# Two layers of a diffusion backbone: the transposes of the attention weights wait for the last head of their block

## The chip, the cores and the metric

The kernel runs on one core of one Trainium2 chip. Its engines are TensorE (PE, with a queue of its own for loading the stationary operand, PEld), VectorE (DVE), ScalarE (ACT), GpSimd (POOL) and SyncE (SP), each of which works through its own list of instructions; DMA queues move the data. The metric is the device time of one execution in microseconds (us), the median of several runs.

## The reference

The program computes two layers over 512 latent tokens and 256 context tokens of width 1024, in single precision. Layer 0 mixes tokens by attention, layer 1 by a bidirectional retention; each is followed by a SwiGLU feed-forward part, and all parts are modulated by a condition vector. The change lies in the attention of layer 0. Sixteen query heads share four key heads. Latent tokens are taken in blocks of 128 queries; a block attends in one softmax to its window of up to 384 latent keys, to all 256 context keys, and to one learned sink value per head:

```python
s_ctx = jnp.einsum('bqkgd,bnkd->bkgqn', qb, k_c, preferred_element_type=jnp.float32) * scale
s_loc = jnp.einsum('bqkgd,bnkd->bkgqn', qb, kb, preferred_element_type=jnp.float32) * scale
s_loc = jnp.where(valid, s_loc, NEG_INF)
sink_col = jnp.broadcast_to(sink_g, s_ctx.shape[:-1] + (1,))
p = jax.nn.softmax(jnp.concatenate([s_ctx, s_loc, sink_col], axis=-1), axis=-1).astype(vb.dtype)
return (jnp.einsum('bkgqn,bnkd->bqkgd', p[..., :L], v_c)
        + jnp.einsum('bkgqn,bnkd->bqkgd', p[..., L:L + band], vb))
```

Context tokens attend to the 256 context keys and the sink alone.

## The kernel before

The attention stage runs over four groups g of four query heads that share a key head, and in each group over six blocks: four of latent queries and two of context queries, 24 blocks in all. `attend(g, s, b)` (line 757) issues one block: `score(i)` for its four heads, `turn(ki)` for each of its two to five key tiles of 128 keys, then `output()`.

- `score(i)`. POOL copies the head's sink value into the last column of a row buffer `pr` (line 687). PE multiplies queries and keys into a PSUM bank (line 703; every product takes two matmuls). DVE adds the mask, stores the row and keeps its extreme (line 704). After each second head DVE scales the extremes of the pair (line 710), ACT takes the exponentials of both rows and sums them (line 101), DVE inverts the sums (line 714), and POOL multiplies each row by its inverse (line 717): this is the normalisation. A block so has two pairs of heads and four normalisations.
- `turn(ki)`. PE transposes the 128 columns of key tile ki of the four rows into one PSUM bank `pT`, of which there are two (line 726). The first of the four transposes takes head 0, then follow heads 2, 1 and 3. ACT or DVE, in turn, copies the bank to SBUF as `tt` (line 728).
- `output()`. PE multiplies the values by `tt`, two products a key tile (line 740). The first ones wait for the last copy of the block, by a dependency that the program states itself (line 742). DVE copies the result out (line 755), or in the last group ACT and DVE split it in two parts at once (lines 164 and 165).

Row buffers: nine of `pr`, so two blocks and one head are in flight; a buffer is free for line 687 of a later block when the last transpose of its row is done.

Between the blocks of a group stand the pieces of `make_q` (lines 559 to 632), which project the queries of the next group: 48 matmuls per pair of heads over the latent and the context tokens (lines 147 to 149). In the last group the output projection of the context tokens stands there instead. They have nothing to do with the block beside them and can fill PE while it waits for a softmax.

The order of each engine's list in this stage is not written out by hand. A planner takes the instructions in the program's order as their rank, follows the dependencies, and puts on each engine what it takes to be ready at that time. An instruction that is ready early by its account, such as the transpose of head 0, is placed early, and on the chip the engine then waits at it for whatever is late. The stages before and after have the same order in both programs.

Of the kernel before, what the change touches and what calls it, by code (L numbers as in the profile page):

```python
# [14 lines left out]
P = 128  # L15
# [34 lines left out]
def dit_kernel(ctx, tc, xT, cT, crow, small, consts, masks, tabs0, tabs1, jtab, adaQ, adaN, adaT, wst, out):  # L50
    nc = tc.nc
    mult, add, sub = ALU.mult, ALU.add, ALU.subtract
# [9 lines left out]
    def T(pool, cols, tag, bufs, dt=F32):  # L62
        return pool.tile([P, cols], dt, tag=tag, bufs=bufs, name=tag)
# [8 lines left out]
    ident, bd = cst[:, 0:128], cst[:, 128:256]  # L72
# [27 lines left out]
    def lnexp(*args, **kw):  # L100
        ins = nc.scalar.activation(*args, **kw)  # L101
        after(ins, [turn["pre"]])
        turn["lnexp"].append(ins)
        return ins
# [150 lines left out]
    def gated_add(s, l, part, d, o, res):  # L255
        return nc.vector.scalar_tensor_tensor(res[d], o, mods[l, s][:, part, d:d + 1], res[d], mult, add)  # L256
# [407 lines left out]
    run_dep = mybir.DependencyInfo(mybir.DependencyClass.Sync, mybir.DependencyReason.DATA)  # L664
# [3 lines left out]
    class Block:  # L668
# [9 lines left out]
        def score(self, i):  # L678
            g, s, b, n = self.g, self.s, self.b, len(self.keys) * P
            hd, nl = 4 * g + i, len(self.lk) * P  # L680
            if i % 2 == 0:
                self.st = T(ap, 16, "stat", 4)
            st, c = self.st, 2 * (b + 4 * s)
            qt = q[hd, s][:, b * P:(b + 1) * P]
            pt = T(ap, 656, "pr", PRB)[:, :n + 1]
            top = stats[hd][:, 1, c + hd % 2:c + hd % 2 + 1]
            nc.gpsimd.tensor_copy(pt[:, n:n + 1], top)
            lo, x0 = st[:, i % 2:i % 2 + 1], self.lk[0] * P if nl else 0

            if nl == 384:  # L690
                runs = [(nl, SC, 5 * P, [(0, SC, kc)]), (0, nl, 2 * P, [(0, nl, kx)])]
            elif nl == 0:
                runs = [(0, SC, 5 * P, [(0, SC, kc)])]
            elif b == 0:
                runs = [(0, n, 3 * P, [(0, nl, kx), (nl, SC, kc)])]
            else:
                runs = [(0, n, 0, [(0, SC, kc), (SC, nl, kx)])]
            for c0, w, m0, parts in runs:
                bank = pS()[:, :w]
                for p0, pw, kk in parts:  # L700
                    for r in range(2):
                        keys = kk[g][r] if kk is kc else kk[g][r][:, x0:x0 + pw]
                        nc.tensor.matmul(bank[:, p0:p0 + pw], qt, keys, start=r == 0, stop=r == 1)  # L703
                nc.vector.tensor_tensor_reduce(pt[:, c0:c0 + w], bank, mask[:, m0:m0 + w], 1.0, top, add, ALU.min, lo)
                top = lo
            self.pr.append(pt)
            if i % 2 == 0:
                return
            y = stats[hd][:, 0, c:c + 2]
            nc.vector.scalar_tensor_tensor(st[:, 2:4], st[:, 0:2], -1.0, y, mult, mult)  # L710
            for e in range(2):
                pt = self.pr[i - 1 + e]
                lnexp(pt, pt, AF.Exp, scale=y[:, e:e + 1], bias=st[:, 2 + e:3 + e], accum_out=st[:, 4 + e:5 + e])
            nc.vector.reciprocal(st[:, 6:8], st[:, 4:6])  # L714
            for e in range(2):
                pt = self.pr[i - 1 + e]
                nc.gpsimd.tensor_scalar(pt[:, :n], pt[:, :n], st[:, 6 + e:7 + e], 1.0, op0=mult, op1=mult)  # L717
            if i == 3:
                self.tt = []

        def turn(self, ki):
            if ki >= len(self.keys):
                return
            tp = pT()
            for a in range(4):
                nc.tensor.transpose(tp[:, a * P:(a + 1) * P], self.pr[(0, 2, 1, 3)[a]][:, ki * P:(ki + 1) * P], ident)  # L726
            tt = T(ap, 512, "tt", TTB)
            self.last = nc.scalar.copy(tt, tp) if ki % 2 == 0 else nc.vector.tensor_copy(tt, tp)
            if ki % 2 == 0:
                self.copy = self.last  # L730
            self.tt.append(tt)
# [83 lines left out]
    def context_out(d, w):  # L815
        o = pj(SC)
        project(w, o_t[1], o)
        ins = gated_add(1, 0, 2, d, o, cres)
        add_square(1, int(d != early[0]), cres[d])
        return ins  # L820
# [37 lines left out]
    for d4 in range(0, KT, 4):  # L858
# [4 lines left out]
        for d in range(d4, d4 + 4):  # L863
            o = pj(SX)
            project(w[d - d4], o_t[0], o)
            ins = gated_add(0, 0, 2, d, o, xr)
# [3 lines left out]
        for d in range(d4, d4 + 4) if d4 else ():  # L870
            ins = context_out(d, w[d - d4])
# [142 lines left out]
    def seven():  # L1014
        g, u = raw_turn(), raw_turn()
        l_, r_ = slice(0, 512), slice(512, 1024)
        b11 = w_parts(fp, 1)
        split(g, *b11)
        t1 = T(fp, 512, "bhi", 1, F32R), T(fp, 512, "blo", 1, F32R)
        nc.vector.tensor_tensor(g[:, l_], u[:, l_], g[:, l_], op=sub)  # L1020
        split(g[:, l_], *t1)
        nc.vector.tensor_tensor(g[:, l_], u[:, r_], g[:, l_], op=sub)
        nc.vector.tensor_tensor(g[:, r_], g[:, r_], g[:, l_], op=sub)
        b24 = w_parts(fp, 1)
        half = split(g, *b24)
        nc.vector.tensor_tensor(u[:, l_], u[:, r_], u[:, l_], op=sub)
        b3 = w_parts(fp, 1)
        split(u, *b3)
        if cr:
            ada_next(half)  # L1030
        X, Y, Z = bank("X"), bank("Y"), bank("Z")
        c11, c12, c22, c21 = t_hn(384), t_hn(384), t_sq(384), t_sq(384)
        a = new_act()
        product(Y, operand["11"], b11, 0, True)
        nc.scalar.copy(c11, Y)
        product(X, operand["12"], b11, 512, True)
        nc.vector.tensor_tensor(c11, c11, X, op=add)
        silu(c11, c11)
        product(Y, operand[2], b24, 0, False)
        nc.scalar.copy(c12, Y)  # L1040
        product(Z, operand[1], t1, 0, True)
        nc.scalar.copy(c21, Z)
        product(Y, operand[3], b3, 0, False)
        nc.scalar.copy(c22, Y)  # L1044
        nc.vector.tensor_tensor(c22, c22, c21, op=add)
        product(Z, operand[4], b3, 512, False)
        nc.vector.tensor_tensor(c12, c12, Z, op=add)
        finish_half(a, 0, c11, c12)
        product(Y, operand["22"], b24, 512, False)
        silu(c21, Y)  # L1050
        return a, finish_half(a, 1, c21, c22)
# [74 lines left out]
    for gsz in FFN_GROUPS:  # L1126
        acts = []
        for i in range(gsz):
# [4 lines left out]
            else:  # L1133
                if f == PLAIN:
                    last_sum()
                a, end = seven()
# [178 lines left out]
    def first_weights_v(hd):  # L1315
        return [split_chunk(chunk(chunk_base + 16 * hd + 4 + i)) for i in range(2)]

    def values_first(w, by_k=False):

        Y = [W4("Z"), W4("Z")]  # L1320
        ins = product_v(Y, quarter_of("11"), w, True, by_k=by_k)
        vt = [T(rp, 512, "res", 12) for _ in range(4)]
        for t in range(2):
            nc.scalar.copy(vt[t], Y[t])
        return w, Y, vt, ins
# [10 lines left out]
    b11, Yv, vt, ins = values_first(b11, True)  # L1336
    normed = context_norm([ins])
    for hd in range(RH):
# [236 lines left out]
        if not last:  # L1575

            b11, Yv, vt, ins = values_first(first_weights_v(hd + 1))
# [7 lines left out]
        def out_tile(d, c, tags="XY"):  # L1585
            while len(w) * 2 <= d:
                w.append(next_w(hpool[0]))
            oo = (W4(tags[d % 2]) if tags[d % 2] != "j" else pj())[:, c]
            for k in range(4):
                c0 = k * 256 + (d % 2) * P  # L1590
                mm3(oo, [p[c0 // 512][:, c0 % 512:c0 % 512 + P] if type(p) is list else p[:, c0:c0 + P]
                         for p in w[d // 2]],
                    (yt[k][0][:, c], yt[k][1][:, c]), k == 0, k == 3)
            return nc.vector.scalar_tensor_tensor(xr[d][:, c], oo, mods[1, 0][:, 2, d:d + 1], xr[d][:, c], mult, add)
# [38 lines left out]
        for i, c in ((0, HALVES[1]), (1, HALVES[0])):  # L1633
            for d in range(KT):
                ins = out_tile(d, c, "XY" if i else "jZ")
# [283 lines left out]
```

## Time and profile before

| what | value |
|---|---|
| median of 3 runs | 1748.62 us (1747.97 to 1750.29) |
| span of the profiled execution, first to last instruction | 1744.4 us |
| instructions in it | 27605 |
| first and last transpose (line 726) | 108.1 us, 315.4 us |
| DMA, mean | 117 GB/s |

The profiled execution is one run, and the page gives its span; the times of runs are taken from outside of it and are 4.2 us longer in the median. In the rows that follow, times are in us unless marked ns; a row of a timeline gives the start, the length, engine, line, operation, what it writes and reads, and in brackets how long the engine stood idle before it and for whom it waited. The ends of matmuls are modelled and overlap the next one, so how fast PE really goes is read from start to start. A row of waits gives the sum, the count and the longest. A row of windows gives, for a stretch, its length and each engine's busy time with its count of instructions, then the granted clock of PE as a share, the share of DMA and its GB/s.

### The profile page before, as it was taken

Reading aid. Unit: us, or ns where it says so; the run is one execution under the profiler, and the core shown is the slowest. Engines: PE = TensorE matmul, PEld = TensorE weight load, DVE = VectorE, ACT = ScalarE, POOL = GpSimd, SP = SyncE. Lnnn points to the kernel's source line nnn. Section 1 sums busy time; section 2 is a strip of 40 time slices with the busy share of each in tenths; the row PEclk is TensorE's granted clock in tenths of the full one; section 3 lists DMA queues with packets and bytes.
Section 4 is the critical chain, followed back from the end, with each engine's and each line's share of the span. In section 5 each row is a group of like instructions: output and inputs, shape, how many; then the busy total and the mean of one; then the engine's idle time right before and its main releaser. Section 6 shows DMA issues by size and latency. Waiting matters only on the chain.

```text
span 1744.4 us, 27605 instructions
## 1 busy us (share of the span) xinstructions
PE 1712.7 (98%) x10876; PEld 1527.8 (88%) x10876; DVE 1350.5 (77%) x2368; ACT 846.3 (49%) x1492; POOL 131.0 (8%) x270
## 2 busy tenths in 40 slices
PE   7999999999999999999999999999999999999999
PEld 5777777899999999999988888898898899999997
DVE  6697778788778788787889858758768798777774
ACT  5576667465433334342456534525525565445442
POOL 0035435000000000000000000000000000000000
PEclk9999999999999999999999999999999999999999
DMA  9501012533243534343423524423423224233322
GB/s 353 230 13 38 13 43 68 204 122 135 71 147 121 158 109 145 123 153 101 156 99 86 182 84 130 162 86 121 157 85 118 76 84 132 77 117 101 104 79 85
DMA packets 59602, 203.54 MB, mean 117 GB/s; under 512 B 6608, under 2 KB 6992, under 8 KB 59216
## 3 DMA queue, kind: packets, MB, share of 16 engines
q1 hardware_dynamic: 51984, 175.03, 30.9%
q0 software_dynamic: 7200, 26.22, 5.2%
q8 instruction: 85, 1.39, 0.3%
q10 hardware_dynamic: 288, 0.52, 0.1%
q14 instruction: 45, 0.37, 0.1%
HBM read 199.65 MB, written 2.10 MB: 116 GB/s over the span
## 4 chain that ended last, share of the span: by engine, by line
PE 80%; DVE 8%; DMA 5%; ACT 3%; issue 2%; POOL 1%; SPq 0%; ACTq 0%; POOLq 0%; DVEq 0%
PE Y L886 15%; PE Z L886 7%; PE pj L147 6%; PE pj L148 6%; PE pj L149 6%; PE Z L1268 6%; PE X L886 4%; PE Y L1257 3%; PE pj L1268 2%; PE pT L726 2%; PE X L1257 2%; DMA wraw<-in_wst_dram 2%; PE pO L740 2%; PE S L703 2%; DMA adan<-in_adaQ_dram 1%
## 5 line engine op out<-in xcount | busy, mean ns | idle before, releaser
L164 ACT CAST whi<-wraw 128x1024 fp32r<-128x1024 f32 x258 | 270.2, 1051 | 370.7 <-PE Z L149 88.5
L165 DVE TENSOR_TENSOR wlo<-wraw,whi 128x1024 fp32r<-128x1024 f32 x258 | 315.0, 1223 | 60.9 <-ACT whi L164 59.7
L886 PE MATMUL Y<-aq,whi 128*128 128x384 f32 x640 | 173.7, 335 | 0.5 <-ACT sq L1044 0.5
L256 DVE SCALAR_TENSOR_TENSOR res<-pj,mod,res 128x512 f32<-128x512 f32 (+1 forms) x112 | 81.5, 729 | 65.6 <-PE pj L149 65.0
L886 PEld LDWEIGHTS Y<-aq,whi 128*128 128x128 f32 x640 | 116.6, 188 | 1.7 <-ACT sq L1044 0.9
L273 DVE CUSTOM_DVE_ANT_0 y<-adaw,crow,small_sb 128x1024 bf16<-128x1024 f32 x64 | 81.9, 1280 | 36.0 <-DMA adaw<-in_adaT_dram 35.7
L886 PE MATMUL Y<-aq,wlo 128*128 128x384 f32 x320 | 107.0, 334 | 0.0
L101 ACT ACTIVATE pr<-pr,stat,qs 128x513 f32<-128x513 f32 (+2 forms) x96 | 74.4, 777 | 23.5 <-DVE stat L710 22.9
L1268 PE MATMUL Z<-whi,sA 128*128 128x512 f32 x256 | 81.0, 391 | 1.2 <-ACT gate L1454 1.2
L717 POOL TENSOR_SCALAR pr<-pr,stat 128x512 f32<-128x512 f32 (+2 forms) x96 | 70.2, 744 | 79.5 <-DVE stat L714 54.8
L147 PE MATMUL pj<-ax,whi 128*128 128x512 f32 x176 | 68.8, 391 | 0.1
L149 PE MATMUL pj<-ax,whi 128*128 128x512 f32 x176 | 68.7, 390 | 0.0
L148 PE MATMUL pj<-ax,wlo 128*128 128x512 f32 x176 | 68.5, 389 | 0.0
L147 PE MATMUL pj<-act,whi 128*128 128x512 f32 x168 | 66.0, 393 | 0.0
L148 PE MATMUL pj<-act,wlo 128*128 128x512 f32 x168 | 65.9, 392 | 0.0
L149 PE MATMUL pj<-act,whi 128*128 128x512 f32 x168 | 65.5, 390 | 0.0
L270 POOL DMA_DIRECT2D adaw<-in_adaT_dram x48 | 25.6, 533 | 514.9 <-DVE mod L273 413.6
L726 PE MATMUL pT<-const_sb,pr 128*128 128x128 f32 x352 | 57.4, 285 | 6.1 <-POOL pr L717 3.6
L886 PE MATMUL Y<-sA,whi 128*128 128x256 f32 x304 | 60.6, 282 | 0.2 <-ACT res L1721 0.2
L886 PEld LDWEIGHTS Y<-aq,wlo 128*128 128x128 f32 x320 | 60.1, 188 | 0.0
L726 PEld LDWEIGHTS pT<-const_sb,pr 128*128 128x128 f32 x352 | 39.1, 142 | 23.0 <-POOL pr L717 12.4
L1268 PEld LDWEIGHTS Z<-whi,sA 128*128 128x128 f32 x256 | 48.0, 188 | 11.7 <-ACT gate L1454 1.9
(576 smaller groups left out, 5150.3 us busy)
## 6 DMA issues: line engine op xcount, KB each, us to landing
wraw<-in_wst_dram SPq DMA_DIRECT2D x224, 512.0 KB, 3.7
adaw<-in_adaT_dram POOLq DMA_DIRECT2D x48, 512.0 KB, 3.9
wx<-in_wst_dram SPq DMA_DIRECT2D x30, 512.0 KB, 4.3
adan<-in_adaQ_dram SPq DMA_DIRECT2D x16, 512.0 KB, 8.5
adan<-in_adaN_dram SPq DMA_DIRECT2D x12, 512.0 KB, 7.8
adaw<-in_adaT_dram SPq DMA_DIRECT2D x8, 512.0 KB, 3.9
res<-in_xT_dram SPq DMA_DIRECT2D x14, 256.0 KB, 3.8
aq<-in_adaN_dram SPq DMA_DIRECT2D x12, 256.0 KB, 5.8
```

What stands on the lines that cost most here:

```text
L101: ins = nc.scalar.activation(*args, **kw)
L147: nc.tensor.matmul(o, whi, xhi, start=first, stop=False)
L148: nc.tensor.matmul(o, wlo, xhi, start=False, stop=False)
L149: return nc.tensor.matmul(o, whi, xlo, start=False, stop=last)
L164: after(nc.scalar.copy(hi, t), behind)
L165: return nc.vector.tensor_tensor(lo, t, hi, op=sub)
L256: return nc.vector.scalar_tensor_tensor(res[d], o, mods[l, s][:, part, d:d + 1], res[d], mult, add)
L273: res.append(nc.vector.tensor_tensor_reduce(junk, w, cr[:, s * 1024:(s + 1) * 1024], 1.0, sm_t[:, C_ADAB + l * 48 + j:C_ADAB + l * 48 + j ...
L726: nc.tensor.transpose(tp[:, a * P:(a + 1) * P], self.pr[(0, 2, 1, 3)[a]][:, ki * P:(ki + 1) * P], ident)
L886: nc.tensor.matmul(o, p, r, start=first and k + i == 0, stop=k == 3 and i == 2, skip_group_check=not first)
L1257: ins = nc.tensor.matmul(o[:, e * SC:(e + 1) * SC], p[:, ws], r, start=first and k + e + i == 0, stop=k == 3 and i == 2, skip_group_check= ...
L1268: ins = nc.tensor.matmul(os[t], p, r, start=first and k + i == 0, stop=k == 3 and i == 2, skip_group_check=by_k or not first)
```

## The change

The last normalisation of a pair is remembered, and each transpose gets a dependency on the one remembered when `turn` is issued, which is that of the block's fourth head. Arithmetic, buffers and the order in which the program issues its instructions stay as they are; the planner makes a new order from them.

```diff
@@ -714,7 +714,7 @@
             nc.vector.reciprocal(st[:, 6:8], st[:, 4:6])
             for e in range(2):
                 pt = self.pr[i - 1 + e]
-                nc.gpsimd.tensor_scalar(pt[:, :n], pt[:, :n], st[:, 6 + e:7 + e], 1.0, op0=mult, op1=mult)
+                self.normed = nc.gpsimd.tensor_scalar(pt[:, :n], pt[:, :n], st[:, 6 + e:7 + e], 1.0, op0=mult, op1=mult)
             if i == 3:
                 self.tt = []
 
@@ -723,7 +723,8 @@
                 return
             tp = pT()
             for a in range(4):
-                nc.tensor.transpose(tp[:, a * P:(a + 1) * P], self.pr[(0, 2, 1, 3)[a]][:, ki * P:(ki + 1) * P], ident)
+                ins = nc.tensor.transpose(tp[:, a * P:(a + 1) * P], self.pr[(0, 2, 1, 3)[a]][:, ki * P:(ki + 1) * P], ident)
+                tc.add_manual_dep(ins.ins, self.normed.ins.name, run_dep, reason="transposes of a tile in one run")
             tt = T(ap, 512, "tt", TTB)
```

`run_dep` (line 664) is the kind of dependency that `output()` uses already: it orders two instructions on different engines as if data passed between them. In the new program every line after 725 is one further down: the copies stand in line 729 and the value products in line 741.

## The prediction

> **What bounds the kernel now.** I read first the busy times of the page and the same in three stretches, to see which engine the end hangs on before, in and after attention.
>
> ```profile
> PE 1712.7 (98%) x10876; PEld 1527.8 (88%) x10876; DVE 1350.5 (77%) x2368; ACT 846.3 (49%) x1492; POOL 131.0 (8%) x270
> ```
>
> ```profile
> core 0: us, PE busy (x) PEld busy (x) DVE busy (x) ACT busy (x) POOL busy (x), PEclk, DMA share, GB/s
> 0.00:97.00 97.00, 83.76 (x893) 66.08 (x894) 65.90 (x159) 51.46 (x98) 3.39 (x12) 1.00 0.71 268
> 97.00:320.00 223.00, 213.56 (x1508) 170.22 (x1507) 174.78 (x551) 155.47 (x367) 94.16 (x199) 0.99 0.12 37
> 320.00:1744.40 1424.40, 1415.42 (x8480) 1291.49 (x8478) 1109.80 (x1659) 639.36 (x1028) 33.41 (x60) 1.00 0.38 119
> ```
>
> TensorE (PE) sets the end: after 320 us it is busy 1415.4 of 1424.4 us, so whatever attention saves or loses between 97 and 320 us passes to the end one for one. All instructions that the change touches lie in those 223 us; before and after them the order of PE's work is the same in both programs. DMA moves at a share of 0.12 there and is no limit.
>
> Then the chain of waits inside the stretch, and what ended the waits of the transposes (line 726):
>
> ```profile
> by line: PE pT L726 16.9%; PE pO L740 12.5%; PE S L703 12.5%; POOL pr L717 7.2%; PE pj L147 6.8%; PE pj L148 6.8%; PE pj L149 6.6%; DVE pr L704 4.8%; ACT pr L101 4.4%; PE pj L610 3.0%; issue 2.6%; DVE tt L728 1.8%; DVE q L601 1.2%; DVE q L6
> ```
>
> ```profile
> L726 PE MATMUL pT<-const_sb,pr x352: 270/273/474, 108.1 to 315.4; 128*128 128x128 f32 x176
> ...
>   POOL pr L717: 16.0, 40
>   ACT tt L728: 5.7, 16
> ```
>
> The 352 transposes wait 40 times, 16.0 us in all, for POOL's normalisation, on the weight-load queue and the matmul queue together. Most of that is hidden, since earlier matmuls still run. PE itself ran empty nine times, 3.6 us, and these are the rows:
>
> ```profile
> 108.14 0.44 PE L726 MATMUL pT<-const_sb,pr 128*128 128x128 f32 x2 [0.40 <-POOL pr L717]
> ...
> 124.19 0.44 PE L726 MATMUL pT<-const_sb,pr 128*128 128x128 f32 x2 [0.55 <-POOL pr L717]
> ...
> 136.14 0.55 PE L726 MATMUL pT<-const_sb,pr 128*128 128x128 f32 x3 [0.72 <-POOL pr L717]
> ...
> 218.41 0.66 PE L726 MATMUL pT<-const_sb,pr 128*128 128x128 f32 x4 [0.23 <-POOL pr L717]
> ...
> 245.32 0.40 PE L147 MATMUL pj<-h,whi 128*128 128x512 f32 x1
> 246.00 0.44 PE L726 MATMUL pT<-const_sb,pr 128*128 128x128 f32 x2 [0.29 <-POOL pr L717]
> 246.20 0.48 PE L148 MATMUL pj<-h,wlo 128*128 128x512 f32 x1
> 246.51 0.40 PE L149 MATMUL pj<-h,whi 128*128 128x512 f32 x1
> ...
> 281.04 0.44 PE L726 MATMUL pT<-const_sb,pr 128*128 128x128 f32 x2 [0.42 <-POOL pr L717]
> 298.83 0.33 PE L726 MATMUL pT<-const_sb,pr 128*128 128x128 f32 x1 [0.45 <-POOL pr L717]
> 303.74 0.44 PE L726 MATMUL pT<-const_sb,pr 128*128 128x128 f32 x2 [0.31 <-POOL pr L717]
> 312.86 1.10 PE L726 MATMUL pT<-const_sb,pr 128*128 128x128 f32 x6 [0.23 <-POOL pr L717]
> ```
>
> Two kinds are mixed. At 108, 246 and 299 us it is an **early run**: the one or two transposes of head 0, issued while the other three heads are still in softmax. At 124, 136, 218, 281, 304 and 313 us it is the **last-head wait**: a run that has begun and stops for the final head.
>
> **The change part by part.** No arithmetic is added or removed. Every transpose gets a wait on the last of the block's four normalisations, and the planner, which now cannot place transposes of head 0 early, orders the attention stage anew. Counted in the two built programs, PE's transposes stand in 77 runs before (18 of two, 9 of one, the others of four and more) and in 52 after (32 of eight, 19 of four, 1 of twenty). 21 of the 24 blocks had an early run; none has one after.
>
> *Early runs go.* What one costs is read from start times, because matmuls overlap. In the fence above, a 512-wide projection matmul starts 0.31 us before the next right after a run (246.20 to 246.51), but the undisturbed pitch is smaller:
>
> ```profile
> 238.77 0.52 PE L703 MATMUL S<-k,q 128*128 128x384 f32 x2
> 239.13 0.39 PE L148 MATMUL pj<-h,wlo 128*128 128x512 f32 x1
> 239.36 0.39 PE L149 MATMUL pj<-h,whi 128*128 128x512 f32 x1
> 239.59 0.40 PE L703 MATMUL S<-kc,q 128*128 128x256 f32 x2
> 239.83 0.39 PE L147 MATMUL pj<-h,whi 128*128 128x512 f32 x1
> 240.15 0.44 PE L726 MATMUL pT<-const_sb,pr 128*128 128x128 f32 x2
> 240.34 0.60 PE L703 MATMUL S<-k,q 128*128 128x384 f32 x2
> 240.78 0.40 PE L148 MATMUL pj<-h,wlo 128*128 128x512 f32 x1
> ...
> 249.56 0.29 PE L147 MATMUL pj<-hc,whi 128*128 128x256 f32 x1
> 249.68 0.82 PE L726 MATMUL pT<-const_sb,pr 128*128 128x128 f32 x6
> 250.26 0.36 PE L148 MATMUL pj<-hc,wlo 128*128 128x256 f32 x1
> 250.46 0.28 PE L149 MATMUL pj<-hc,whi 128*128 128x256 f32 x1
> ```
>
> A 512-wide matmul takes 0.23 us (239.13 to 239.36), two 384-wide ones 0.36 us (238.77 to 239.13). From 249.56 to 250.46 six transposes stand between two 256-wide matmuls of half a 512's pitch each; 0.90 - 0.23 leaves 0.67 us, 0.11 us per transpose, with nothing for the change of work. The early run at 240.15 stands in 239.83 to 240.78, 0.95 us; less 0.23, 0.36 and 2 x 0.11 leaves 0.14 us lost, without any row of idle time. The one at 246.00, which did wait, stands in 245.32 to 246.51, 1.19 us; less 2 x 0.23 and 2 x 0.11 leaves 0.51 us. So 21 early runs cost between 21 x 0.14 = 2.9 and 21 x 0.51 = 10.7 us. Three show idle time, so I take 3 x 0.51 + 18 x 0.14 = 4.1 us saved.
>
> *Other run starts.* 25 runs fewer, 21 of them the early ones: 4 x 0.14 = 0.6 us saved; 0 if they cost as little as the run of six.
>
> *The two transposes of head 0 move behind the last normalisation.* PE does them in either case, 0.22 us. They cost only where PE used to run empty before the last head, in the six last-head rows: 6 x 0.22 = 1.3 us lost. If every block paid, 24 x 0.22 = 5.3 us.
>
> *The last-head wait itself.* A run that stopped between the third and the fourth head now starts only after the fourth, up to one normalisation later:
>
> ```profile
> L717 POOL TENSOR_SCALAR pr<-pr,stat x96: 473/693/2054, 106.9 to 312.8; 128x512 f32<-128x512 f32 x32, 128x640 f32<-128x640 f32 x32, 128x256 f32<-128x256 f32 x32
> ```
>
> Median 0.69 us. But its end is the same instant, and the planner now puts other work before it: counted at the pitches above, PE has on average 6.5 us of work between a block's last score and its first transpose; before, 6.0 us lay between that score and the third. I take zero. The bounds: all six last-head rows vanish, 2.46 us idle, or all 24 blocks wait a whole normalisation longer, 24 x 0.69 = 16.6 us.
>
> *Queues.* Behind a waiting run on PE stand the next blocks' scores and projections; behind those, VectorE's masks (line 704) and ScalarE's exponentials. On POOL the sink-column copies (line 687) need the row buffers that the transposes release:
>
> ```profile
> POOL pr L687 <- PE pT L726: 34.3, 23, 3.7
> ```
>
> In several blocks such a copy stood between the two pairs of normalisations and held the second pair; in the new order the four normalisations of a block stand together more often and the copies follow. I price that at nothing: POOL is busy 94 of 223 us. VectorE and ScalarE keep their instructions and are busy 175 and 155 of 223 us. On SP one modulation load of 512 KB trades places with weight loads; at a DMA share of 0.12 it hides, and uncovered it is one landing, 3.7 us (page, DMA issues).
>
> ```profile
> wraw<-in_wst_dram SPq DMA_DIRECT2D x224, 512.0 KB, 3.7
> ```
>
> Sum: -4.1 - 0.6 + 1.3 = -3.4 us. The profiled span is 1744.4 us, 4.2 us under the median of the timed runs, 1748.62; I carry those 4.2 us along: span 1741.0, time 1745.2 us. A measurement here tells about 0.2%, 3.5 us, from no change, so the forecast lies on that edge.
>
> The Trainium skill, page "TensorE: Matmul & The Clock Gate", section "Part 2: What happens when you issue a matmul", says that PE may load weights ahead of running matmuls but keeps matmuls in program order. The trace agrees: at 246.00 the matmul of 246.20 stood behind a waiting transpose. By that rule an early transpose that waits holds back all work after it.
>
> **The rivals.** *Slower: the whole run waits on POOL.* POOL's normalisation holds 7.2% of the chain in 223 us, 16.1 us, or 23 operations of 0.69: about one per block lies on the path already. Where PE has no filler, a block now pays 0.69 + 0.22 = 0.91 us. If half of the 24 blocks do, 12 x 0.91 = 10.9 us against 4.7 saved: +6.2 us, 1754.8 us. It decides over 0.2% slower from (3.5 + 4.7) / 0.91 = 9 blocks. For it: in the last head group little projection work is left. Against: only six blocks ran empty there before.
>
> *Hidden: the gain comes back as waits.* PE arrives sooner and waits longer for VectorE and POOL; only the clearest three early waits are saved, 1.5 us, less 1.3: 1748.4 us. For it: VectorE is the busiest beside PE. Against: most of the 40 waits are hidden already.
>
> *More: early runs all cost as at 246.00.* 10.7 saved, 1.3 lost: 1739.2 us. Against: only three show idle time.
>
> *The half clock.* Around the start of the last head group PE was thinly fed, and the granted clock fell:
>
> ```profile
> 255.00:270.00 15.00, 12.59 (x83) 9.21 (x81) 13.26 (x49) 11.65 (x32) 5.01 (x12) 0.89 0.12 36
> ```
>
> 15 x 0.11 = 1.7 us. Moving transposes later could bring a second such dip, 1746.7 us, or remove this one, 1743.3 us; both stay near the forecast. The page named above, section "HAM oscillation", has the clock halve after idle windows; it would make longer gaps between runs cost more than the gap.
>
> That the change does nothing is excluded: the order of PE's work differs from the first block on.
>
> **How the numbers follow.** Forecast, with the clock dip either way, 1742 to 1748: 0.45. Larger gain, 0.19. Hidden, 0.10. Slower, 0.26. Faster by over 0.2% (below 1745.1): the larger gain and half of the forecast's share, 0.42. Within: the other half and hidden, 0.32. Slower: 0.26. Cases of both signs hold much of the chance, so the range leaves out only the tails beyond the larger gain and the slow rival: 1738.5 to 1755.0.
>
> **What would show it.** Right: no transpose run of one or two; fewer than 40 waits of line 726 for line 717; PE's idle rows at line 726 at most the six last-head ones; the stretch from the first score to the last value product some 3 us shorter. Wrong: "PE pT" rows with idle times near 0.7 us in ten or more blocks, waits of scores or value products behind them, a second dip of the clock after 250 us, or line 717's share of the chain above 10%.

## The result and the profile after

The changed kernel takes 1751.57 us in the median of 20 runs (1749.75 to 1753.27), the kernel before 1748.47 us on the same chip (1746.44 to 1751.32, 20 runs). The ratio is 1.0016, with a 95% interval of 1.001 to 1.0022: slower by 3.1 us, or 0.16%. Run again later beside other kernels it gave 1751.16 us against 1748.61 us, ratio 1.0014 (1.0005 to 1.0023). The forecast was 1745.2 us. The time lies in the range that was given and on the other side of no change.

The busy times in the same three stretches, of the changed kernel (columns as before):

```profile
core 0: us, PE busy (x) PEld busy (x) DVE busy (x) ACT busy (x) POOL busy (x), PEclk, DMA share, GB/s
0.00:97.00 97.00, 86.09 (x892) 67.14 (x893) 65.99 (x159) 51.57 (x98) 3.23 (x12) 0.98 0.71 268
97.00:320.00 223.00, 208.91 (x1478) 170.65 (x1477) 171.57 (x545) 151.91 (x360) 95.80 (x199) 0.98 0.12 35
320.00:1750.30 1430.30, 1420.70 (x8512) 1294.60 (x8509) 1112.25 (x1664) 642.23 (x1035) 33.41 (x60) 1.00 0.38 119
```

The loss sits where the change sits. From 97 to 320 us TensorE is busy 208.91 us where it was 213.56, and 30 matmuls fewer fit in; they follow after 320 us, where TensorE is as full as before. The first score of the stage and its last value products, in the kernel before:

```profile
98.58 0.80 PE L703 MATMUL S<-k,q 128*128 128x256 f32 x2
...
316.51 1.95 PE L740 MATMUL pO<-tt,v 128*64 128x256 f32 x16
```

and with the change:

```profile
98.64 0.81 PE L703 MATMUL S<-k,q 128*128 128x256 f32 x2
...
322.65 1.95 PE L741 MATMUL pO<-tt,v 128*64 128x256 f32 x16
```

The start is the same, though the granted clock ahead of it was 0.98 and not 1.00; the end is 6.1 us later. These are two single executions; the medians lie 3.1 us apart.

The chain of waits in that stretch, and what ended the waits of the transposes:

```profile
by line: PE pT L726 13.4%; POOL pr L717 13.1%; PE pO L741 11.9%; DVE pr L704 10.8%; ACT pr L101 8.3%; PE S L703 8.3%; issue 4.2%; POOL hn L590 3.6%; PE pj L147 2.8%; PE pj L149 2.5%; DVE tt L729 2.4%; PE pj L610 2.3%; PE pj L148 2.2%; DVE h
```

```profile
L726 PE MATMUL pT<-const_sb,pr x352: 270/273/478, 115.4 to 321.5; 128*128 128x128 f32 x176
...
  POOL pr L717: 22.4, 31
  DVE tt L729: 3.1, 6
```

GpSimd's normalisation (line 717) went from 7.2% to 13.1% of the chain, and the softmax ahead of it (lines 704 and 101) from 9.2% to 19.1%. The transposes wait for it less often, 31 times instead of 40, but 22.4 us instead of 16.0. The first transpose comes 7 us later (115.4 instead of 108.1): the early runs are gone. PE itself ran empty at them 14 times, 8.6 us, instead of 9 times, 3.6 us (sum, count, longest):

```profile
PEld pT L726 <- POOL pr L717: 13.8, 17, 1.7
PE pT L726 <- POOL pr L717: 8.6, 14, 1.5
```

Some of these rows; each is the first transpose of its block, with seven more in line behind it:

```profile
124.27 1.97 PE L726 MATMUL pT<-const_sb,pr 128*128 128x128 f32 x8 [1.37 <-POOL pr L717]
...
193.97 1.09 PE L726 MATMUL pT<-const_sb,pr 128*128 128x128 f32 x8 [1.00 <-POOL pr L717]
...
216.83 1.09 PE L726 MATMUL pT<-const_sb,pr 128*128 128x128 f32 x8 [0.58 <-POOL pr L717]
...
308.71 1.09 PE L726 MATMUL pT<-const_sb,pr 128*128 128x128 f32 x8 [1.14 <-POOL pr L717]
```

In this profile the granted clock fell at two places of the stage instead of one:

```profile
120.00:130.00 10.00, 8.25 (x46) 6.22 (x44) 7.79 (x20) 4.38 (x11) 4.03 (x10) 0.83 0.16 52
255.00:270.00 15.00, 12.04 (x73) 9.36 (x72) 11.17 (x40) 10.41 (x27) 6.12 (x12) 0.81 0.12 32
```

So three readings stood open: theory W, that the wait on the last head costs; theory O, that the planner's new order costs; theory C, that the half clock does. Each kernel below was timed in five rounds against the kernel before on the same chip; an interval is 0.09 to 0.14% wide to either side, 1.6 to 2.4 us.

### The profile page after: what moved, and what is told of

Same layout as the page of the kernel before. It is cut to its first block, busy times and chain, and to the rows that moved or that the text cites. A ratio compares the mean times of both kernels' runs of the same rounds, so it can differ in the third digit from the quotient of the medians.

```text
span 1750.3 us, 27616 instructions
## 1 busy us (share of the span) xinstructions
PE 1715.7 (98%) x10876; PEld 1532.4 (88%) x10876; DVE 1349.8 (77%) x2368; ACT 845.7 (48%) x1492; POOL 132.4 (8%) x270
## 3 DMA queue, kind: packets, MB, share of 16 engines
q1 hardware_dynamic: 51984, 175.03, 31.2%
## 4 chain that ended last, share of the span: by engine, by line
PE 75%; DVE 12%; DMA 5%; ACT 4%; issue 3%; POOL 2%; SPq 0%; ACTq 0%; DVEq 0%; POOLq 0%
PE Y L887 14%; PE Z L887 7%; PE pj L147 6%; PE pj L149 6%; PE pj L148 6%; PE Z L1269 5%; PE X L887 3%; DMA wraw<-in_wst_dram 3%; PE Y L1258 2%; DVE wlo L165 2%; PE X L1258 2%; PE pj L1269 2%; PE pT L726 2%; POOL pr L717 2%; PE pO L741 2%
## 5 line engine op out<-in xcount | busy, mean ns | idle before, releaser
L270 POOL DMA_DIRECT2D adaw<-in_adaT_dram x48 | 25.6, 533 | 514.0 <-DVE mod L273 413.5
L726 PE MATMUL pT<-const_sb,pr 128*128 128x128 f32 x352 | 52.1, 289 | 9.9 <-POOL pr L717 8.6
L704 DVE CUSTOM_DVE_ANT_0 pr<-S,mask,qs 128x256 f32<-128x256 f32 (+1 forms) x96 | 52.8, 566 | 7.8 <-PE S L703 6.3
```

Source lines behind the costliest of these rows:

```text
L726: ins = nc.tensor.transpose(tp[:, a * P:(a + 1) * P], self.pr[(0, 2, 1, 3)[a]][:, ki * P:(ki + 1) * P], ident)
```

## The experiments

### The wait weakened or put elsewhere

First, the same dependency as one of order alone, which the planner obeys and the chip doesn't wait for:

```diff
-tc.add_manual_dep(ins.ins, self.normed.ins.name, run_dep, reason="transposes of a tile in one run")
+tc.add_manual_dep(ins.ins, self.normed.ins.name, order, reason="transposes of a tile in one run")
```

> The dependency of each transpose on the last normalisation becomes one that only the planner sees; on the chip a transpose waits for its own head's row alone. The planner's order comes out close to that of the changed kernel, not equal: the runs start somewhat earlier, and five of them are cut. Theory W (the loss comes from PE waiting empty for the last normalisation): PE's idle rows at line 726 for line 717 fall from the changed kernel's 8.6 us to below 5 us and the time is at most that of the kernel before, 1746 to 1748.5 us. Theory O (the new order of the other work costs, not the wait): as the changed kernel, 1751 to 1752 us.

Measured: 1748.57 us, ratio 1.0002 (0.9993 to 1.0011), and 4.6 us of idle rows, as W expected. No loss without the wait. But the planner made a third order out of it, neither that of before nor that of after, so this alone doesn't part W from O.

Then the full wait in the last group of heads only, and in the first three only:

```diff
+if self.g == NKV - 1:
     tc.add_manual_dep(ins.ins, self.normed.ins.name, run_dep, reason="transposes of a tile in one run")
```

> The wait in the last head group alone (8 of the 24 blocks by the numbers of the trace, from about 258 us on), where little projection work is left to fill PE. By the two traces the end of the third group is 3.4 us later in the changed kernel and the end of attention 6.1 us. Theory W with the price where filler is missing: most of the loss stays, ratio to before 1.001 to 1.002 (1750 to 1752 us). If the price is paid by blocks anywhere: less than half of it stays, ratio 1.0000 to 1.0008.

> The complement: the wait in the first three head groups, the last group as before. Theory W with the price where filler is missing: ratio 0.999 to 1.0005, the removed early runs showing as a gain. If the price is paid by blocks anywhere: ratio 1.0008 to 1.0016. Theory O gives no number for either half; the two need not add up to the whole.

Measured: 1748.52 us, ratio 0.9999 (0.999 to 1.0008), for the last group; 1751.19 us, 1.0015 (1.0006 to 1.0024), for the first three (`if self.g < NKV - 1`). The last group, with the least projection work to fill in, loses nothing that can be told, where W with the price at missing filler had most of the loss. So a lack of filler alone doesn't make the loss.

The first two groups singly:

> The change in the blocks of the first group of heads alone. Theory W, by the idle time at the transposes for normalisations, which goes from 4.6 to 5.5 us between 97 and 165 us: at most 0.9 us slower, 1748.5 to 1749.5 us. Theory O: a third of what the first three groups cost together, 2.7 us: 0.9 us. Theory C (half clock): 1.7 us where the clock falls between 120 and 130 us, nothing where it doesn't.

> The change in the blocks of the second group alone. Theory W: here the idle time at the transposes for normalisations goes from 1.7 to 6.2 us between 165 and 212 us, so most of the loss of the first three groups should sit here: 2 to 4 us slower, 1750.5 to 1752.5 us. Theory O: a third of 2.7 us, so 1749.4 us. Theory C: no half-clock stretch lies there, so 1748.5 us.

Measured: 1748.86 us, ratio 0.9999 (0.999 to 1.0008), and 1749.22 us, 1.0002 (0.9993 to 1.0011). The 2 to 4 us that W put into the second group did not come. Together the two are 0.9 us at most by their medians, and the three groups 2.7 us. With 1.6 us to either side such parts can't be added up, so these runs don't tell where in the stage the loss lies.

The wait moved to the third head, and to the second, whose normalisation ends earlier:

```diff
+if i == 1:
+    self.second = self.normed
...
-tc.add_manual_dep(ins.ins, self.normed.ins.name, run_dep, reason="transposes of a tile in one run")
+tc.add_manual_dep(ins.ins, self.second.ins.name, run_dep, reason="transposes of a tile in one run")
```

> Each transpose waits for the third head's normalisation in place of the fourth's, one POOL operation (0.69 us median) earlier; the fourth transpose of a tile still waits for its own row. Theory W: blocks that ran empty lose less; of 14 PE rows with 8.6 us idle about half remains, and the time is 1748 to 1750 us. Theory O: 1751 to 1752 us or anything else, since the planner makes yet another order.

> The change, but the transposes of a key tile wait for the normalisation of the block's second head only. Theory W (the time is lost because the first transpose of a block now stands behind the normalisation of the last head, which GpSimd ends late): the second row is long done when the transposes come, so no loss: 1748.5 us, ratio 0.9990 to 1.0010, and TensorE waits for GpSimd at the transposes no more than in the kernel before (3.6 us over 97 to 325 us). Theory O (the added dependencies alone, by the order they bring about, cost it): 1751 us, ratio about 1.0016. Theory C (the loss is the granted clock, which falls where TensorE stands still): as W, with one half-clock stretch in the attention as before.

Measured: third head 1749.29 us, ratio 1.0001 (0.9992 to 1.001); second head 1752.37 us, 1.0024 (1.0015 to 1.0033), as slow as the change itself, where W expected nothing. What ended the waits of the transposes (line 728 there) with the second head:

```profile
L728 PE MATMUL pT<-const_sb,pr x352: 270/273/447, 110.0 to 321.7; 128*128 128x128 f32 x176
...
  POOL pr L717: 25.6, 46
```

Here the planner still places runs early, the first at 110.0 us, and they now wait for the second row instead of the first: 46 waits, 25.6 us. So W, as it stood, was too narrow: what matters is not only which row is waited for, but where the planner puts the waiting instruction. Whether order or wait costs the 3.5 us of this kernel was not taken apart.

### The wait made longer, and taken away

One more GpSimd operation on the last row, a multiplication by 1.0, which the transposes wait for:

```diff
+self.normed = nc.gpsimd.tensor_scalar(pt[:, :n], pt[:, :n], ones[:, 0:1], 1.0, op0=mult, op1=mult)
```

> The change with one more GpSimd multiplication (by 1.0) on the last head's row, which the transposes wait for: it makes the wait longer by one operation of 0.69 us in each of the 24 blocks. Theory W: the wait is exposed in about 14 blocks (14 waits of TensorE for the normalisation in the trace after), so 14 x 0.69 = 9.7 us more than the changed kernel: about 1761 us, ratio 1.005 to 1.008 to the kernel before. Theory O (order, not the wait): at most the GpSimd work beside, 1751 to 1753 us. Theory C: as W plus 1.7 us for each further half-clock stretch of 3.4 us; more than three such stretches in the attention and a mean clock under 0.995.

Measured: 1765.78 us, ratio 1.0096 (1.0083 to 1.011), 14 us above the changed kernel. At 0.69 us each that would be 21 of the 24 blocks, more than the 14 rows in which TensorE ran empty. The waits of the transposes grew by about as much:

```profile
  POOL pr L719: 38.2, 39
```

22.4 to 38.2 us is 15.8 us. What theory C expected came too: the mean clock of these runs is 0.994, under 0.995, so a part of the 14 us is the half clock and the blocks are fewer than 21. In most blocks, even so, the moment at which the last row is ready is on the path, or comes onto it when it is 0.69 us later.

The normalisation left out, in both kernels; the rows stay unnormalised, and in the second kernel the transposes wait for the last head's exponential instead:

```diff
-nc.gpsimd.tensor_scalar(pt[:, :n], pt[:, :n], st[:, 6 + e:7 + e], 1.0, op0=mult, op1=mult)
+pass
```

> The kernel before without the normalisation of the rows (the 96 GpSimd multiplications are left out, so the rows stay unnormalised). It is the base for the next run. Theory W: faster than before by the waits for the normalisation that TensorE has (7.4 us by start-to-start gaps): about 1741 us. Theory O: the same.

> The changed kernel without the normalisation of the rows (left out as in the run before it); the transposes wait for the last head's exponential instead. Theory W: with GpSimd's 0.69 us and its start out of the way the wait behind the last head is shorter by about 1 us, and of the 3.1 us between the two kernels under 1 us is left: within 0.06% of the run before it. Theory O (starting the transposes of a block late costs by itself, whatever is waited for): the 3 us are still there. Theory C: no half-clock stretch beyond those of the run before it.

Measured: 1743.07 us, ratio 0.9968 (0.9956 to 0.9981), and 1743.85 us, 0.9971 (0.996 to 0.9983). The gap between the two programs is gone, within what can be told. All that the normalisations cost the kernel before is 5.8 us, the difference of the first to 1748.89 in that comparison.

The last head's normalisation on VectorE, in both kernels:

```diff
-nc.gpsimd.tensor_scalar(pt[:, :n], pt[:, :n], st[:, 6 + e:7 + e], 1.0, op0=mult, op1=mult)
+(nc.vector if i + e == 4 else nc.gpsimd).tensor_scalar(pt[:, :n], pt[:, :n], st[:, 6 + e:7 + e], 1.0, op0=mult, op1=mult)
```

> The changed kernel, with the normalisation of a block's last head on VectorE instead of GpSimd, so that the last two rows of a block are normalised side by side and the row that the transposes wait for is ready about 0.69 us earlier. Theory W (TensorE pays for the normalisation on which the run of transposes hangs, by as much as it is late): 9 to 14 waits shorter by up to 0.69 us, so 3 to 6 us less than the changed kernel: 1746 to 1749 us, idle time at the transposes for normalisations under 16 us. Theory O (the order costs, not the latency): 1751 us or more. In both VectorE has 24 operations of up to 0.8 us more, some 16 us of the 223 us stage, of which it is idle 22%; if they come before the reading of scores, up to 2 us of that come back.

> The kernel before with the same move of the last head's normalisation to VectorE. Theory W: its waits are mostly for the first heads, which GpSimd still normalises, so it gains less than the changed kernel does: 1746 to 1749 us, and the gap between this run and the one before it is under 1 us. Theory O: the gap of 3 us stays.

Measured: with the change 1753.73 us, ratio 1.0033 (1.0021 to 1.0044); without it 1749.43 us, 1.0007 (0.9997 to 1.0016). Both expectations of W fell: the gap stays, at 4.3 us. The waits of the transposes in the kernel with the change:

```profile
PEld pT L726 <- POOL pr L717: 5.1, 8, 1.9
...
PE pT L726 <- DVE pr L717: 4.0, 4, 1.6
```

The idle time shrank to 9.9 us and the loss did not. So idle time at the transposes is no price list. By then order and wait had never been changed one at a time.

### The order held, the wait alone taken out or put in

The next kernel takes the program before and binds each TensorE instruction of the stage to its predecessor in the changed kernel's list, by dependencies of order alone (`ORDER` holds the 1279 names; `seen` keeps the instructions as they are issued). Only VectorE's list differs from the changed kernel's, by two neighbours.

```diff
+keep = mybir.DependencyInfo(mybir.DependencyClass.NoSync, mybir.DependencyReason.DATA)
+line = ["I-%d" % n for n in ORDER]
+for p0, p1 in zip(line, line[1:]):
+    tc.add_manual_dep(seen[p1].ins, p0, keep, reason="order of TensorE")
```

> The kernel before, with TensorE's instructions of the stage held to the changed kernel's order by dependencies that bind the order alone, each on its predecessor; the transposes wait for no more than their own row. ScalarE's and GpSimd's lists come out as in the changed kernel too, VectorE's but for two instructions side by side, so that the wait on the last head is all that is missing. Theory W (the wait): the 3 us are gone, 1747.5 to 1749.5 us; idle time at the transposes for normalisations 1 to 5 us under the changed kernel's 22.4 us. Theory O (the order): the 3 us stay, 1750.5 to 1752.5 us.

> The changed kernel once more, beside the two runs above on the same chip. Both theories: 1751.5 us, ratio 1.001 to 1.0022.

Measured: the order without the wait 1745.73 us, ratio 0.9982 (0.9974 to 0.9991); the changed kernel on the same chip 1751.16 us, 1.0014. So the new order alone gains 2.9 us, and the wait alone costs 5.4 us on top of it. Theory O falls. W had expected 1747.5 us or more and saw no gain in the order. The idle time at the transposes fell by 11.8 us where W had 1 to 5; their waits (line 785 there) without the wait on the last head:

```profile
  POOL pr L776: 10.6, 21
```

The reverse, the changed kernel held to the order of before, so that the early runs of head 0 wait for the last head:

> The changed kernel with TensorE's instructions of the stage held to the order of the kernel before: the transposes of head 0 that stood early in 21 blocks stay there and now wait for the last head. Theory W: the wait without the new order is dearer than with it, as the early runs wait for the whole softmax of the last pair: 21 x 0.7 us or more, so at least 1763 us. Theory O: with the old order there is no loss, 1748.5 us.

Measured: 1818.83 us, ratio 1.0405 (1.0391 to 1.0419). The wait in the old order costs 70 us, at a mean clock of 0.983; its transposes wait for normalisations this long:

```profile
  POOL pr L775: 119.9, 37
```

That the change costs only 3 us is the planner's doing, which moves the runs back.

What the wait costs is seen at one place, the ninth block. GpSimd's run of four normalisations (the first two are the third and fourth head of this block, the other two belong to the tenth) and TensorE's transposes behind it, with the change:

```profile
191.45 4.27 POOL L717 TENSOR_SCALAR pr<-pr,stat 128x640 f32<-128x640 f32 x4 [0.85 <-DVE stat L714]
```

```profile
193.97 1.09 PE L726 MATMUL pT<-const_sb,pr 128*128 128x128 f32 x8 [1.00 <-POOL pr L717]
```

and the same in the same order without the wait:

```profile
188.04 4.28 POOL L776 TENSOR_SCALAR pr<-pr,stat 128x640 f32<-128x640 f32 x4 [0.85 <-DVE stat L773]
```

```profile
189.39 0.84 PE L785 MATMUL pT<-const_sb,pr 128*128 128x128 f32 x3
190.57 0.76 PE L785 MATMUL pT<-const_sb,pr 128*128 128x128 f32 x5 [0.34 <-POOL pr L776]
...
196.57 2.38 PE L799 MATMUL pO<-tt,v 128*64 128x256 f32 x20
```

From the start of GpSimd's run to the end of the wait it is 2.52 us with the change (193.97 less 191.45) and 2.53 us without (190.57 less 188.04): the last row is ready at the same moment. But then eight transposes follow in one case and five in the other, because three, those of heads 0, 2 and 1, had begun before the last row was ready. The block's value products start 8.53 us after the start of GpSimd's run (196.57 less 188.04), and with the change 8.85 us after it (200.30 less 191.45):

```profile
200.30 2.38 PE L741 MATMUL pO<-tt,v 128*64 128x256 f32 x20
```

That is 0.32 us in this block, three transposes of 0.11. In the trace without the wait, 18 of the 24 blocks have transposes that start before the last row of their block is ready, 47 transposes in all. How much of this delay reaches the end of the stage is read further down, from whole traces.

Last, the same order with the wait on the third of a tile's four transposes, so that one transpose moves behind the last normalisation instead of three, and the kernel without the wait again beside it:

```diff
+if a == 2:
+    tc.add_manual_dep(ins.ins, self.normed.ins.name, run_dep, reason="transposes of a tile in one run")
```

> The changed kernel's order held as in the run without the wait, and the wait on the last head put on the third of a tile's four transposes instead of on all: the first two (heads 0 and 2) may run as soon as their rows are ready, one (head 1) stands behind the last normalisation instead of three. If the price of the wait is the transposes that it moves behind the normalisation (about 5.4 us for three), one costs a third: 1.8 us more than the run without the wait, 1746.5 to 1748.5 us. If it is the waiting itself, whatever stands behind it, the whole 5.4 us: 1750.5 to 1752 us.

> The changed kernel's order without the wait once more, on the same chip as the run above: 1744.5 to 1747 us, ratio 0.9974 to 0.9991 to the kernel before.

Measured: 1747.84 us, ratio 0.9997 (0.9988 to 1.0005), and 1746.36 us, 0.999 (0.9981 to 0.9999). By the medians one transpose behind the wait costs 1.5 us and three cost 5.4, or 4.2 to 5.9 by the ratios of the two comparisons of each (0.9982 and 0.999 without the wait, 1.0014 and 1.0016 with it). In the ninth block:

```profile
188.96 4.26 POOL L776 TENSOR_SCALAR pr<-pr,stat 128x640 f32<-128x640 f32 x4 [0.84 <-DVE stat L773]
```

```profile
190.32 0.72 PE L785 MATMUL pT<-const_sb,pr 128*128 128x128 f32 x2
191.48 0.87 PE L785 MATMUL pT<-const_sb,pr 128*128 128x128 f32 x6 [0.45 <-POOL pr L776]
```

Two before the wait and six after it, and again 2.52 us to its end. A difference of 1.5 us is no more than the intervals; what it does exclude is the whole 5.4 us.

The traces tell it more sharply, as TensorE works through the same list in the first five of these profiles. From the start of the first score to the start of the last value products, in us, with the granted clock in two stretches:

| kernel | first score | last value products | between them | clock, 120 to 130 us | clock, 255 to 270 us |
|---|---|---|---|---|---|
| changed, first profile | 98.64 | 322.65 | 224.01 | 0.83 | 0.81 |
| changed, second profile | 98.94 | 321.71 | 222.77 | 1.00 | 0.80 |
| its order, wait on the third transpose | 98.51 | 319.15 | 220.64 | 1.00 | 0.77 |
| its order, no wait | 97.89 | 317.43 | 219.54 | 1.00 | 0.77 |
| its order, no wait, again | 98.24 | 316.41 | 218.17 | 1.00 | 0.89 |
| before | 98.58 | 316.51 | 217.93 | 1.00 | 0.89 |

The second, third and fourth rows have the clock dip in common, 0.77 to 0.80 over 15 us. There three transposes behind the wait cost 3.23 us (222.77 less 219.54) and one costs 1.10 (220.64 less 219.54): ten times 0.32 and ten times 0.11 us. Net, the delay of ten blocks reaches the end, out of the 18 with such transposes. So the price of the wait at an equal clock is the transposes that it puts behind the last row, and not the waiting as such. The timed runs have 1.0 to 2.7 us more; the next part comes to that.

The order without the wait is faster than both kernels, by 0.18% and 0.10% against the kernel before in its two comparisons. That gain rests on the timed runs alone: the last two rows, with equal dips, show none of it (218.17 and 217.93), and that profile of the kernel before was 2.4 us quicker than its median.

### The half clock

Theory C needs no kernel of its own, as each run comes with its granted clock. The second profile of the changed kernel has the dip after 255 us, and none at 120 to 130 us:

```profile
120.00:130.00 10.00, 8.24 (x58) 5.61 (x56) 9.20 (x25) 5.58 (x14) 4.25 (x10) 1.00 0.19 52
255.00:270.00 15.00, 11.90 (x69) 8.99 (x69) 11.65 (x40) 10.20 (x26) 6.18 (x13) 0.80 0.12 36
```

So what a dip costs can be read between two runs of one program. In the first profile the transposes of the second block start at 124.27 us (in the rows above), and the next value products at

```profile
129.86 2.38 PE L741 MATMUL pO<-tt,v 128*64 128x256 f32 x20
```

which is 5.59 us later. In the second profile they start at 124.49 and 128.67 us, 4.18 us apart. The dip cost 1.4 us. By its row, 10 us at 0.83, it took 1.7 us of clock. The Trainium skill, page "TensorE: Matmul & The Clock Gate", section "HAM oscillation", counts half of the throttled time as lost. At the clock of 0.50 that the trace shows from 125 to 127 us that is the whole 1.7 us, an estimate by the page; the trace comes near it with 1.4.

The order without the wait dips in its profile too, after 255 us as deep as the changed kernel:

```profile
120.00:130.00 10.00, 8.79 (x60) 5.64 (x57) 9.52 (x25) 5.63 (x13) 3.43 (x6) 1.00 0.15 54
255.00:270.00 15.00, 12.64 (x71) 8.87 (x69) 12.09 (x46) 10.27 (x29) 6.09 (x12) 0.77 0.12 36
```

The kernel that waits for the third head has a mean clock of 0.9965 over 11 runs, as low as the changed kernel's 0.9966, and no loss to be told; the one that waits for the second head has 0.998, as the kernel before, and loses 3.5 us. So the clock alone isn't what parts slow from fast. But it has a share. The changed kernel's mean clock is 0.0014 under that of its order without the wait (0.9966 and 0.9967 against 0.9980 and 0.9981). That is 2.4 us of 1748, and about 2 us if it costs as the dip above did; 3.2 and 2 are 5.2 us, within the 4.2 to 5.9 that were timed. This is an estimate: the mean clock of a timed run doesn't say where its dips lie. Where they lie matters, as the clock of 0.98 ahead of the stage left its start where it was. That may be why the mean clock says little of the time of a run: among the runs of one and the same changed or tried kernel (179 runs of 18 series), a mean clock lower by 0.001, 1.7 us, goes with 0.52 us more, give or take 0.12; among the 118 runs of the kernel before with 0.09, give or take 0.16. Against the kernel before, the changed one lies 0.0015 lower: 0.8 us of the 3.1 by the larger slope, 2.2 by the dip that was traced.

## Why the prediction was wrong

- **What bounds the kernel.** Right: the loss arose in the stage and came through to the end.
- **Early runs go, other run starts.** Right in sign by the timed runs, and too large. Put at -4.1 and -0.6 us; the order alone, which holds all of both, gained 2.9 us and 1.6 us in two comparisons.
- **The two transposes of head 0 move behind the last normalisation.** Too small in two ways. Not two transposes move but up to three, those of heads 0, 2 and 1, as the middle of a run had used the wait for the last row. And it is not six blocks that pay: 18 of the 24 have transposes to move, and ten blocks' worth of the delay reaches the end. The count of six was taken from the idle rows of the old order. (One of the six was misread: the run at 312.86 us waited for the third head, whose row ends at 312.81, and not for the last.)
- **The last-head wait itself.** This is the step that failed. It was taken as zero, because the end of the wait is the same instant and because on average 6.5 us of other work stood before the first transpose, instead of 6.0 before the third. The first half is true, to 0.01 us in the ninth block. It doesn't follow that the wait is free: what was done during it now comes after it. And the mean work ahead says nothing of the blocks in which it doesn't reach. This step and the one before, +1.3 us together, measured 3.2 us in the traces at an equal clock, and 4.2 to 5.9 us in the timed runs, with the half clock's share in it. Against 1.6 to 2.9 us of gain where 4.7 were put, the sum changes its sign.
- **Queues.** Nothing in the runs speaks against pricing them at zero: the sink copies wait for the transposes 31.2 us in the order without the wait and 36.0 us with it, and 34.3 us before. What had to be priced at GpSimd was not its load but the moment of its last result, as the doubled operation showed.
- **From span to time.** The 4.2 us carried along mixed two things. Time less span of one and the same run is 1.75 us (1752.05 for the changed kernel's profiled 1750.3); the profiled run of before was simply 2.4 us quicker than the median. On the median 1748.5 the same sum would have given 1745.1, so this moved nothing.
- **The rivals.** *Slower* had the right side and half of the mechanism. It put 0.91 us on each of 12 blocks, 0.69 of it for a longer normalisation; that part didn't come, as the end of the wait stayed where it was, and the transposes behind it, put at 0.22, cost 0.32 us. *Hidden* had the gain come back as waits for VectorE and GpSimd and stopped at no change; the waits came, for GpSimd, and went past it. *The half clock* came true as a second dip in one of the two profiles, and its price was about right, 1.7 us put and 1.4 traced; but a dip more beside the forecast gain isn't what happened. (1745.2 us with 1.7 more or less is 1746.9 and 1743.5, not 1746.7 and 1743.3.) *More* fell: the order alone gained 2.9 us at best, not 10.7.
- **The signs.** Of those set down for "wrong", the chain's share above 10% and, in one profile, the second dip came; idle rows of 0.58 us or more for line 717 came six times and not ten. Of those set down for "right", two came as well: no transpose run shorter than four, and 31 waits instead of 40. They told of the order and not of its price. The other two failed: 14 idle rows for line 717 and not six, and a stage 6.1 us longer in the profiles instead of 3 us shorter.

## What to carry to other kernels

On an engine that works in order, a wait moved to the head of a run costs what the run used to do while waiting: count the instructions that pass behind it and the blocks in which the engine stands there after the change, not before it. A dependency that is added for order's sake can be split in two, order alone and wait alone, and the two tried singly: here the order was worth 1.6 to 2.9 us in timed runs, the wait cost 4.2 to 5.9, and keeping the one without the other beats both kernels. And where two programs hold an engine to one list, their traces can be laid side by side instruction by instruction: that told 1.1 us from 3.2, where the times had 1.6 us of noise.

## What the runs showed of the hardware

- What a dip of the granted clock costs goes by where it lies. Inside the stage 10 us at 0.83 cost 1.4 us of the 1.7 us of clock that they took. Ahead of the stage, 97 us at 0.98 left the first score at 98.64 us, against 98.58 at 1.00. So the mean clock of a run tells little of its time: the kernel before averaged 1748.4 us in 23 runs at 0.997, 1749.1 in 51 at 0.998, and 1748.3 in 41 at 0.999.
- One profiled execution can stand as far off as the effect looked for: that of the kernel before was 2.4 us quicker than its median, that of the kernel waiting for the second head 4.8 us slower than its own (1757.2 us against 1752.37). A difference of 0.2% in the span can't be read from one trace each; the parts of a stage can, where the order is the same.
- VectorE normalises some rows faster than GpSimd, not all. Both at work on rows of 640 at the same moment, in the kernel that has the change and gives VectorE the last head:

```profile
191.45 1.16 POOL L717 TENSOR_SCALAR pr<-pr,stat 128x640 f32<-128x640 f32 x1 [1.53 <-DVE stat L710]
```

```profile
191.39 0.55 DVE L717 TENSOR_SCALAR pr<-pr,stat 128x640 f32<-128x640 f32 x1
```

This pair is one of GpSimd's slower ones. In that trace the medians are 0.35, 0.70 and 0.55 us on VectorE for rows of 256, 512 and 640, and 0.48, 0.70 and 0.81 us on GpSimd. The move gained nothing for the program: 1749.43 us without the change, the same within the interval, and 1753.73 us with it.
